# One 8 KB gather for both rows of an expert, and its gelu formed expert by expert

## The chip, the cores and the metric

The kernel runs on one core of a Trainium2 chip. The metric is the device time of one execution in microseconds (us); lower is better. Three runs of the kernel before took 3461.32, 3467.48 and 3471.10 us, the median is 3467.48 us.

## The reference

512 tokens of 1024 features in float32 go through three transformer blocks. The part that the change touches is the end of the second block, a layer of 16,384 experts of which every token uses 128 (8 heads times 16). Cut to that part:

```python
q  = (h @ wq).reshape(T, 8, 2, 128)
s1 = einsum('thd,hkd->thk', q[:, :, 0], keys1);  s2 = ...keys2
v1, i1 = top_k(s1, 16);  v2, i2 = top_k(s2, 16)        # per head
score, pos = top_k(all sums v1[i] + v2[j], 16)         # 16 of 256
ids   = take(i1 * 128 + i2, pos);   gates = softmax(score)
act   = gelu(einsum('pd,phkd->phk', h, expert_u[ids]))  # 128 dot products of 1024 per token
out   = einsum('phk,phkd->pd', gates * act, expert_v[ids])
```

`gelu` is the form with the hyperbolic tangent: 0.5 x (1 + tanh(0.79788 (x + 0.044715 x^3))). Each token needs 128 rows of `expert_u` and 128 rows of `expert_v`, each 4 KB, 512 x 256 x 4 KB = 537 MB in all.

## The kernel before

The 512 tokens are four tiles of 128, two to a half. The halves run one behind the other: while the experts of half 0 are gathered and summed, half 1 runs the rest of the first block and the mixer of the second; while the experts of half 1 run, half 0 runs its third block (`experts`, L1761). Weights come in 512 KB tiles over the SP queue into six buffers (`wtile`, L206). The experts of a half are a list of steps, `self.fill`. Whenever a phase of the other half asks for PSUM or a weight tile, `tick` (L130) adds credit and takes steps off the list, so that the expert steps are spread between the phase's instructions. This fixes one order of instructions, and each engine goes through its own part of it in that order. The pace is set by tables written out by hand (`ZONE`, `COURSE`), in which each expert step costs 1.46 units.

For one token tile, `gather_steps` (L1155) makes 256 steps: 128 u steps and 128 v steps. A step first calls `run_ahead`, which issues gathers up to 8 steps ahead (`AHEAD`). A gather (`fetch`, L1164) is an indirect DMA issued by GpSimd (POOL): 128 rows of 4 KB, one for each token, into one of the `GB` = 15 buffers named `gu`. Three of these hold other things: `h2` of the two tiles and the running sum `acc`.

A u step (L1171) is one VectorE (DVE) instruction that multiplies the gathered u rows with the activations `h2` and sums over 1024 into one column of `act`. After each 16 u steps (one head) ScalarE (ACT) takes the gelu of the 16 columns at once (L1174) and VectorE multiplies them with the gates (L1175). A v step adds c times the gathered v rows to the sum, c being a column of `act`: mostly VectorE does this (L1194); for a share of the steps that the phase sets, ScalarE builds a diagonal matrix `dg` from c (L1186, two buffers) and TensorE (PE) adds two products to PSUM (L1188). The order is 16 u steps, then u and v alternate with v 16 experts behind, then 16 v steps. `finish` (L1196) adds the two sums up and normalises.

The expert numbers and gates come from `route_steps` (L1242), two heads at a time; the softmax of the gates has an exp on ScalarE (L1294). `peer_route` (L1061) merges the steps of the routing with those of the experts.

Of the kernel before, what the change touches and what calls it, by code (L numbers as in the profile page):

```python
# [21 lines left out]
NT = 4          # token tiles  # L22
NH = 2          # token tiles of a half: the halves run one behind the other
# [34 lines left out]
class Ker:  # L58
    def __init__(self, ctx, tc, I):
# [3 lines left out]
        self.exact = False      # products in float32 itself, not in parts  # L63
# [14 lines left out]
        self.aux = nc.gpsimd        # for what VectorE need not do, unless GpSimd has transfers to start  # L78
# [3 lines left out]
        # states: of the first and of the second block, then both of the third block's retention  # L82
# [42 lines left out]
    def course(self, i):  # L125
        """the rate that spreads the steps of the experts over a phase"""
# [18 lines left out]
    def idle(self, d):  # L145
        """TensorE has little to do for d: pieces of the feed-forward set aside go in between"""
# [29 lines left out]
    def rsqrt(self, out, in_, scale, eps):  # L176
        """out = (in_ * scale + eps) ** -0.5: Newton's iteration from the halved exponent"""
# [43 lines left out]
    def ahead(self):  # L221
        """of the weights of a feed-forward set aside, split the next tile and load on"""
# [9 lines left out]
    def whole(gen):  # L232
        """all pieces of a generator at once; its value"""
# [12 lines left out]
    def g_fm(self, srcs):  # L246
        """feature-major blocks: out[f, i, t] = sum_k w_i[k, f] X[t, k]; srcs [128, 8*128]"""
# [16 lines left out]
    def g_tm(self, srcs, lhs, evac):  # L264
        """token-major: out[t, c] = sum_k lhs[k, t] w[k, c]; srcs: list of [128, 2, 512]; lhs(k) -> (H, L) [128, 512]"""
# [23 lines left out]
    def stats(self, y):  # L289
        """mean and variance over the free axis (1024 or 512)"""  # L290
# [12 lines left out]
    def g_transpose_x(self, src, scale=None, bias=None):  # L303
        """XH, XL <- split of (src^T * scale + bias); src(t, k) -> [128 t, 128 feat]"""
# [756 lines left out]
    def peer_route(self, rate):  # L1061
# [8 lines left out]
        with ExitStack() as e2:  # L1070
# [45 lines left out]
            def each(sc, h):  # L1116
# [5 lines left out]
                if h == 0:  # L1122
                    segs[0][0][0][2]()
# [31 lines left out]
    def gather_steps(self, t, y, h2, idx, gate):  # L1155
# [12 lines left out]
        def u_step(s, g):  # L1168
            if s == 0:
                begin()  # L1170
# [783 lines left out]
```

## Time and profile before

| | |
|---|---|
| median of three runs | 3467.48 us |
| span of the profiled execution | 3464.7 us, 44842 instructions |
| PE busy | 3023.7 us (87%) |
| DVE busy | 2667.9 us (77%) |
| POOL busy | 1439.0 us (42%) |
| ACT busy | 1145.3 us (33%) |
| DMA moved | 957.10 MB, mean 276 GB/s |

Busy time counts an engine's instructions, not the time in which it waits; a busy PE is not PE at its peak, since matmuls overlap. The profile gives no time for the profiled execution other than its span, which lies within the three runs. The expert stretch, from the first gather at 965 us to the last at 2861 us, is seen in the slices of the page: POOL is busy only there, and the DMA engines are at 0.9 or more in most slices of it.

### The profile page before, as it was taken

What the parts mean: (1) busy time and instruction counts of PE and PEld (TensorE: products, weight loads), DVE (VectorE), ACT (ScalarE), POOL (GpSimd) and SP (SyncE); (2) the same over time, 40 slices, a digit from 0 to 9 for tenths busy, and PEclk for the clock granted to TensorE, in tenths of its full rate; (3) what the DMA queues carried; (4) which work ended last, traced back from release to release, by engine and by line L of the source; (5) the groups of instructions that cost most, each with busy time, mean ns of one, the idle gap of its engine ahead of it and who ended that gap; (6) DMA issues with size and microseconds to landing.
All of it is one profiled execution on the core that took longest, in us unless ns stands there. A gap on an engine that the chain in (4) does not pass through costs nothing. (4 is left out here: it accounts for less than half of the span.)

```text
span 3464.7 us, 44842 instructions
## 1 busy us (share of the span) xinstructions
PE 3023.7 (87%) x15402; PEld 2350.9 (68%) x15402; DVE 2667.9 (77%) x6456; ACT 1145.3 (33%) x1687; POOL 1439.0 (42%) x1187
## 2 busy tenths in 40 slices
PE   9999999998979789987777867879797975999998
PEld 9987889888866357836354643536474745888897
DVE  7779686665588999878898999897877786566555
ACT  4454544553312242103222121112222213455554
POOL 0020000023245656655677567586767671211200
PEclk9999999999999899998899988899998987999999
DMA  8863477542389979998999899999999995644365
GB/s 312 279 194 118 131 267 233 168 161 86 105 303 357 355 263 384 409 402 325 381 326 375 335 339 391 347 368 357 333 365 359 396 409 193 182 133 139 119 188 162
DMA packets 276757, 957.10 MB, mean 276 GB/s; under 512 B 38304, under 2 KB 42144, under 8 KB 276528
## 3 DMA queue, kind: packets, MB, share of 16 engines
q0 software_dynamic: 147456, 536.94, 41.0%
q1 hardware_dynamic: 129072, 417.29, 35.6%
q8 instruction: 122, 2.00, 0.2%
q14 instruction: 107, 0.88, 0.1%
HBM read 947.81 MB, written 2.10 MB: 274 GB/s over the span
## 5 line engine op out<-in xcount | busy, mean ns | idle before, releaser
L1164 POOL DMA_INDIRECT gu<-in_peer_v,idx x512 | 633.6, 1238 | 317.1 <-issue 111.9
L1164 POOL DMA_INDIRECT gu<-in_peer_u,idx x512 | 609.3, 1190 | 349.6 <-issue 110.9
L1171 DVE SCALAR_TENSOR_TENSOR gu<-gu 128x1024 f32<-128x1024 f32 x512 | 620.7, 1218 | 59.4 <-DMA gu<-in_peer_u,idx 55.7
L203 DVE TENSOR_TENSOR wL<-wr,wH 128x1024 fp32r<-128x1024 f32 x332 | 409.1, 1234 | 249.2 <-ACT wH L202 231.9
L256 PE MATMUL ps<-XH,wr 128*128 128x256 f32 x2368 | 528.7, 383 | 0.2 <-issue 0.2
L256 PEld LDWEIGHTS ps<-XH,wr 128*128 128x128 f32 x2368 | 450.9, 192 | 73.2 <-issue 12.8
L202 ACT CAST wH<-wr 128x1024 fp32r<-128x1024 f32 x332 | 348.3, 1050 | 440.3 <-PE ps L281 217.4
L1194 DVE SCALAR_TENSOR_TENSOR gu<-gu,act 128x1024 f32<-128x1024 f32 x366 | 467.6, 1278 | 28.6 <-DMA gu<-in_peer_v,idx 23.4
L1188 PE MATMUL ps<-gu,dg 128*128 128x512 f32 x568 | 306.5, 664 | 101.8 <-DMA gu<-in_peer_v,idx 67.4
L1188 PEld LDWEIGHTS ps<-gu,dg 128*128 128x128 f32 x568 | 112.7, 212 | 206.9 <-issue 158.2
L278 PE MATMUL ps<-wr,XH 128*128 128x512 f32 x512 | 229.1, 601 | 0.0
L256 PE MATMUL ps<-XH,wH 128*128 128x256 f32 x1408 | 206.5, 289 | 16.3 <-ACT XH L116 10.0
L256 PE MATMUL ps<-XH,wL 128*128 128x256 f32 x1408 | 202.4, 287 | 1.5 <-DVE wL L203 1.2
L256 PE MATMUL ps<-XL,wH 128*128 128x256 f32 x1408 | 203.0, 288 | 0.2
L256 PEld LDWEIGHTS ps<-XH,wH 128*128 128x128 f32 x1408 | 186.6, 196 | 21.9 <-ACT XH L116 13.7
L256 PEld LDWEIGHTS ps<-XH,wL 128*128 128x128 f32 x1408 | 185.6, 196 | 2.9 <-DVE wL L203 2.7
L203 DVE TENSOR_TENSOR fL<-fr,fH 128x1024 fp32r<-128x1024 f32 x98 | 126.1, 1288 | 79.5 <-ACT fH L202 50.1
L256 PEld LDWEIGHTS ps<-XL,wH 128*128 128x128 f32 x1408 | 186.5, 197 | 0.6 <-DVE XL L118 0.6
L278 PEld LDWEIGHTS ps<-wr,XH 128*128 128x128 f32 x512 | 98.0, 193 | 122.7 <-issue 120.3
L202 ACT CAST fH<-fr 128x1024 fp32r<-128x1024 f32 x98 | 102.6, 1047 | 175.4 <-PE ps L256 58.7
L1186 ACT ACTIVATE dg<-ident,act 128x128 f32<-128x128 f32 x142 | 55.1, 400 | 312.3 <-PE ps L1188 246.5
L184 POOL TENSOR_TENSOR r<-rx,mhalf 128x1 f32<-128x1 f32 x18 | 11.9, 669 | 330.7 <-DVE rx L182 330.7
(618 smaller groups left out, 5462.4 us busy)
## 6 DMA issues: line engine op xcount, KB each, us to landing
wr<-in_wi_fm SPq DMA_DIRECT2D x112, 512.0 KB
wr<-in_wi_tm SPq DMA_DIRECT2D x96, 512.0 KB
wr<-in_wf SPq DMA_DIRECT2D x96, 512.0 KB
wr<-in_wo SPq DMA_DIRECT2D x64, 512.0 KB
wa<-in_wada SPq DMA_DIRECT2D x48, 512.0 KB
wr<-in_f2g SPq DMA_DIRECT2D x44, 512.0 KB
wr<-in_f2u SPq DMA_DIRECT2D x44, 512.0 KB
wr<-in_f2d SPq DMA_DIRECT2D x44, 512.0 KB
```

What stands on the lines that cost most here:

```text
L184: nc.gpsimd.tensor_tensor(out=out, in0=x, in1=self.mhalf[:p, :].to_broadcast(list(out.shape)), op=ALU.pow)
L202: self.nc.scalar.copy(H, raw)
L203: self.nc.vector.tensor_tensor(out=L, in0=raw, in1=H, op=ALU.subtract)
L256: nc.tensor.matmul(ps[:, i * TH:(i + 1) * TH], a[:, k * P:(k + 1) * P], b[:, k, :], start=n == 0, stop=n == KD * len(terms) - 1)
L278: nc.tensor.matmul(pss[t], lh[:, ts], wh, start=k == 0, stop=k == nk - 1)
L1164: nc.gpsimd.indirect_dma_start(out=g, out_offset=None, in_=I[src], in_offset=bass.IndirectOffsetOnAxis(ap=idx[:, s:s + 1], axis=0))
L1171: nc.vector.scalar_tensor_tensor(g, g, 1.0, h2, op0=ALU.mult, op1=ALU.mult, accum_out=st["act"][:, s:s + 1])
L1186: nc.scalar.activation(dg, self.ident, AF.Copy, scale=c)
L1188: nc.tensor.matmul(st["ps"][i], dg, g[:, i * 512:(i + 1) * 512], start="pe" not in st, stop=s == 127)
L1194: nc.vector.scalar_tensor_tensor(st["acc"], g, c, st["acc"], op0=ALU.mult, op1=ALU.add)
```

## The change

The two tables `expert_u` and `expert_v` are laid side by side on the host, one row of 8 KB for each expert. One gather brings both rows of an expert (128 rows of 8 KB, 1 MB), into one of 7 buffers of 8 KB for each partition; `h2` and `acc` have buffers of their own (`hb`, 4). `AHEAD` is 4 gathers.

The two tiles of a half are one list of 256 experts. Step u of expert i is followed by step v of expert i - 2 (`LAG`). The coefficient of each expert is formed by itself right after its u step: POOL multiplies the dot product x with the gate (`xg`), and ACT forms x squared, then x + 0.044715 x^3, the tangent, and c = xg (1 + th). The half that gelu needs goes into the gates: the sum of the softmax is doubled (one more VectorE instruction for two heads).

To make room, the tile `acc` of the first block's convolution is taken after the pool of `_hgrn` is closed, and the tiles `X3` of the third block are taken after `block3_mix` instead of before. The tables of the pace are the same. Comments are dropped.

```diff
-AHEAD = 8           # gathers under way ahead of their use
-GB = 15             # their buffers
+AHEAD = 4
+GB = 7
+LAG = 2
+GELU = (0.7978845608028654, 0.044715)
...
-        h2 = [pp.tile([P, D], F32, name="gu", bufs=GB) for _ in range(NH)]
+        h2 = [pp.tile([P, D], F32, name="hb", bufs=4) for _ in range(NH)]
...
-        def fetch(src, s):
-            g = pp.tile([P, D], F32, name="gu", bufs=GB)
-            nc.gpsimd.indirect_dma_start(out=g, out_offset=None, in_=I[src],
-                                         in_offset=bass.IndirectOffsetOnAxis(ap=idx[:, s:s + 1], axis=0))
-            return g
...
+        def fetch(i):
+            g = pp.tile([P, 2 * D], F32, name="gu", bufs=GB)
+            nc.gpsimd.indirect_dma_start(out=g, out_offset=None, in_=I["peer_uv"],
+                                         in_offset=bass.IndirectOffsetOnAxis(
+                                             ap=idx[i // P][:, i % P:i % P + 1], axis=0))
+            live[i] = [g, None]
+
+        def run_ahead(i):
+            while st.get("got", 0) <= min(i + AHEAD, NH * P - 1):
+                fetch(st.get("got", 0))
+                st["got"] = st.get("got", 0) + 1
...
-            nc.vector.scalar_tensor_tensor(g, g, 1.0, h2, op0=ALU.mult, op1=ALU.mult, accum_out=st["act"][:, s:s + 1])
-            if s % 16 == 15:
-                ah = st["act"][:, s - 15:s + 1]
-                nc.scalar.activation(ah, ah, AF.Gelu_apprx_tanh)
-                nc.vector.tensor_tensor(out=ah, in0=ah, in1=gate[:, s // 16, :], op=ALU.mult)
...
+        def u_step(i):
+            run_ahead(i)
+            t, s = divmod(i, P)
+            g = live[i][0]
+            a = pp.tile([P, 6], F32, name="ax", bufs=8)
+            x, q, z, th, xg, c = (a[:, k:k + 1] for k in range(6))
+            nc.vector.scalar_tensor_tensor(g[:, 0:D], g[:, 0:D], 1.0, h2[t], op0=ALU.mult, op1=ALU.mult, accum_out=x)
+
+            nc.gpsimd.tensor_tensor(out=xg, in0=x, in1=gate[t][:, s // 16, s % 16:s % 16 + 1], op=ALU.mult)
+            nc.scalar.activation(q, x, AF.Square, scale=math.sqrt(GELU[1]))
+            nc.scalar.activation(z, x, AF.Identity, scale=q, bias=x)
+            nc.scalar.activation(th, z, AF.Tanh, scale=GELU[0])
+            nc.scalar.activation(c, th, AF.Identity, scale=xg, bias=xg)
+            live[i][1] = c
...
+        steps, at = [], {}
+        for i in range(NH * P + LAG):
+            at[i] = len(steps)
+            if i < NH * P:
+                steps.append((DMA, lambda i=i: u_step(i)))
+            j = i - LAG
+            if j >= 0:
+                steps.append((DMA, lambda j=j: v_step(j)))
+                if j % P == P - 1:
+                    steps.append((FINISH, lambda t=j // P: finish(y[t])))
...
+            nc.vector.tensor_scalar(sm, sm, 2.0, None, op0=ALU.mult)
...
-    o["peer_u"], o["peer_v"] = n["peer_u_2"][0], n["peer_v_2"][0]
+    o["peer_uv"] = np.concatenate([n["peer_u_2"][0], n["peer_v_2"][0]], axis=1)
```

## Rows read from the trace of the kernel before

**Rows 1.** Stretches: length, busy us (count) by engine, PEclk, DMA share, GB/s.
```profile
1213.00:1300.00 87.00, 73.89 (x279) 49.33 (x278) 82.47 (x211) 37.92 (x83) 47.06 (x41) 0.92 0.75 264
...
1386.00:1473.00 87.00, 87.00 (x395) 74.71 (x394) 70.60 (x262) 13.75 (x18) 54.41 (x42) 1.00 1.03 409
...
953.00:2860.00 1907.00, 1585.88 (x6138) 1052.08 (x6136) 1653.23 (x4945) 412.18 (x759) 1241.52 (x1023) 0.91 0.95 358
```

**Rows 2.** DMA queues of the whole span: packets, MB, share of 16 engines.
```profile
q0 software_dynamic: 147456, 536.94, 41.0%
q1 hardware_dynamic: 129072, 417.29, 35.6%
q8 instruction: 122, 2.00, 0.2%
```

**Rows 3.** Costliest groups of the page: count, busy us, mean ns, idle before.
```profile
L1164 POOL DMA_INDIRECT gu<-in_peer_v,idx x512 | 633.6, 1238 | 317.1 <-issue 111.9
L1164 POOL DMA_INDIRECT gu<-in_peer_u,idx x512 | 609.3, 1190 | 349.6 <-issue 110.9
L1171 DVE SCALAR_TENSOR_TENSOR gu<-gu 128x1024 f32<-128x1024 f32 x512 | 620.7, 1218 | 59.4 <-DMA gu<-in_peer_u,idx 55.7
...
L1194 DVE SCALAR_TENSOR_TENSOR gu<-gu,act 128x1024 f32<-128x1024 f32 x366 | 467.6, 1278 | 28.6 <-DMA gu<-in_peer_v,idx 23.4
```

**Rows 4.** Waits from 1040 to 2860 us: total us, times, longest us.
```profile
ACT act L1174 <- DVE gu L1171: 253.8, 21, 56.5
ACT dg L1186 <- PE ps L1188: 228.9, 71, 13.0
...
POOL gu L1164 <- issue: 215.8, 644, 3.2
...
POOL gu L1164 <- DVE gu L1171: 77.0, 36, 12.5
...
DVE gu L1171 <- DMA gu<-in_peer_u,idx: 55.7, 46, 16.5
...
PE ps L1188 <- DMA gu<-in_peer_v,idx: 41.9, 9, 9.8
...
POOL gu L1164 <- DVE gu L1194: 34.2, 28, 4.3
...
POOL gu L1164 <- PE ps L1188: 31.6, 21, 4.4
...
DVE gu L1194 <- DMA gu<-in_peer_v,idx: 23.4, 34, 1.3
```

**Rows 5.** POOL in order of time: start, length us, idle before.
```profile
976.99 0.94 POOL L1164 DMA_INDIRECT gu<-in_peer_u,idx  x1 [0.30 <-issue]
```

**Rows 6.** Groups of instructions on ACT, shapes kept apart: count, busy us, mean ns.
```profile
L1174 ACT ACT_TABLE_LOAD x26 | 33.4, 1283 | 0.5
...
L1294 ACT ACT_TABLE_LOAD x14 | 18.0, 1283 | 0.2
...
L316 ACT ACTIVATE XH<-ps,bf,gf 128x256 f32<-128x256 f32 x16 | 7.5, 576 | 7.5 <-PE ps L310 7.5
...
L316 ACT ACTIVATE XH<-ps,n2w 128x256 f32<-128x256 f32 x8 | 3.4, 471 | 1.0 <-PE ps L310 1.0
...
L1428 ACT ACTIVATE mxo<-mxo,cb 128x16 f32<-128x16 f32 x12 | 3.1, 302 | 4.9 <-DVE mxo L1426 4.9
...
L878 ACT ACTIVATE bt<-ab 128x8 f32<-128x8 f32 x2 | 0.4, 208 | 0.0
```

**Rows 7.** Groups of instructions on POOL with few columns.
```profile
L184 POOL TENSOR_TENSOR r<-rx,mhalf 128x1 f32<-128x1 f32 x18 | 11.9, 669 | 330.7 <-DVE rx L182 330.7
...
L1058 POOL IOTA io<- 128x50 f32 x1 | 0.2, 187 | 0.0
```

**Rows 8.** The gates' multiplication on DVE, 1040 to 2860 us.
```profile
L1175 DVE TENSOR_TENSOR act<-act,gate 128x16 f32<-128x16 f32 x31 | 5.3, 170 | 4.5 <-ACT act L1174 4.5
```

More of the change, by code (lines that the diff above doesn't have):

```diff
@@ L467, in mixer1 @@
                 uT = cvp.tile([P, 4, 30 + TH], F32, name="uT")
-                acc = cvp.tile([P, 4, TH], F32, name="acc")
                 with ExitStack() as e3:
                     hp = e3.enter_context(tc.tile_pool(name="m1h", bufs=1))
-                    self._hgrn(hp, uT, acc)
-                self._conv31(cvp, uT, acc)
+                    self._hgrn(hp, uT)
+                with ExitStack() as e3:
+                    cvp = e3.enter_context(tc.tile_pool(name="m1a", bufs=1))
+                    self._conv31(cvp, uT, cvp.tile([P, 4, TH], F32, name="acc"))
             for c in range(2):
@@ L525, in _conv31, with _hgrn @@
         self.idle(GAP["l"])
-    def _hgrn(self, hp, uT, acc):
+    def _hgrn(self, hp, uT):
         nc, I = self.nc, self.I
@@ L1065, in peer_route @@
         self.rate, self.credit = rate, 0.0
-        h2 = [pp.tile([P, D], F32, name="gu", bufs=GB) for _ in range(NH)]
-        idx = [pp.tile([P, 128], U32, name=f"idx{t}") for t in range(NH)]
-        gate = [pp.tile([P, 8, 16], F32, name=f"gate{t}") for t in range(NH)]
-        segs = [self.gather_steps(t, self.x[:, self.tg(t), :], h2[t], idx[t], gate[t]) for t in range(NH)]
+        h2 = [pp.tile([P, D], F32, name="hb", bufs=4) for _ in range(NH)]
+        idx = [pp.tile([P, 128], U32, name=f"idx{t}", bufs=1 + t) for t in range(NH)]
+        gate = [pp.tile([P, 8, 16], F32, name=f"gate{t}", bufs=1 + t) for t in range(NH)]
+        segs, begin = self.gather_steps([self.x[:, self.tg(t), :] for t in range(NH)], h2, idx, gate)
         with ExitStack() as e2:
@@ L1122, in each @@
                 if h == 0:
-                    segs[0][0][0][2]()
+                    begin()
             nxt = scores(0, each)
@@ L1134, in peer_route @@
                         nxt = scores(1)
-                        self.fill += segs[0][0]
+                        self.fill += segs[0]
                         continue
                     rest[t].append(self.route_steps(g, sc[:, t, :, :], idx[t], gate[t]))
-        self.pop(len(self.fill) - len(segs[0][0]))
+        self.pop(len(self.fill) - len(segs[0]))
         u = self.merge(rest[0][1], self.fill)
         for g in (2, 3):
-            u += self.merge(rest[0][g], segs[0][g - 1])
-        last = segs[0][3][-17:]
-        u += self.merge(sum(rest[1], []), segs[0][3][:-17])
-        b = sum(segs[1], [])
-        self.fill = u + [f for p in zip(last[:16], b[:16]) for f in p] + b[16:20] + last[16:] + b[20:]
+            u += self.merge(rest[0][g], segs[g - 1])
+        self.fill = u + self.merge(sum(rest[1], []), segs[3]) + segs[4]
     @staticmethod
@@ L1180, in v_step @@
                 st["ps"] = [self.psum(), self.psum()]
-            c = st["act"][:, s:s + 1]
+                st["pe"] = False
             self.vcredit += self.vshare
-            if (self.vcredit >= 1.0 and s) or s == 127:
+            if (self.vcredit >= 1.0 and s) or s == P - 1:
                 self.vcredit -= 1.0
@@ L1186, in v_step @@
                 nc.scalar.activation(dg, self.ident, AF.Copy, scale=c)
-                for i in range(2):
-                    nc.tensor.matmul(st["ps"][i], dg, g[:, i * 512:(i + 1) * 512],
-                                     start="pe" not in st, stop=s == 127)
+                for k in range(2):
+                    nc.tensor.matmul(st["ps"][k], dg, g[:, k * 512:(k + 1) * 512],
+                                     start=not st["pe"], stop=s == P - 1)
                 st["pe"] = True
@@ L1208, in finish @@
             nc.vector.scalar_tensor_tensor(y, y, r, fw, op0=ALU.mult, op1=ALU.mult)
-        order = [(u_step, "peer_u", s) for s in range(16)]
-        for h in range(8):
-            for k in range(16):
-                if h < 7:
-                    order.append((u_step, "peer_u", 16 * (h + 1) + k))
-                order.append((v_step, "peer_v", 16 * h + k))
-        ahead = []
-        def run_ahead(i):
-            while len(ahead) < len(order) and len(ahead) <= i + AHEAD:
-                ahead.append(fetch(*order[len(ahead)][1:]))
-        def step(i):
-            run_ahead(i)
-            order[i][0](order[i][2], ahead[i])
-            ahead[i] = None
-        steps = [(DMA, lambda i=i: step(i)) for i in range(len(order))] + [(FINISH, finish)]
-        steps[0] += (lambda: run_ahead(0),)
-        cut = [0, 48 - 2 * AHEAD, 112 - 2 * AHEAD, 176 - 2 * AHEAD, len(steps)]
-        return [steps[a:b] for a, b in zip(cut, cut[1:])]
+        steps, at = [], {}
[8 more added lines that the diff above has]
+                    steps.append((FINISH, lambda t=j // P: finish(y[t])))
+        cut = [0] + [at[32 * k - AHEAD] for k in (1, 2, 3, 4)] + [len(steps)]
+        return [steps[a:b] for a, b in zip(cut, cut[1:])], lambda: run_ahead(0)
     def top16(self, src, val, idx, n):
@@ L1783, in experts @@
             last = self.ctx.enter_context(ExitStack())
-            self.exact = False
-            self.xt(last, "right")
-            X3 = self.XH, self.XL
-            self.exact = True
             with ExitStack() as es:
@@ L1790, in experts @@
                 self.block3_mix()
+                X = self.XH, self.XL
+                self.exact = False
+                self.xt(last, "right")
+                X3 = self.XH, self.XL
+                self.exact = True
+                self.XH, self.XL = X
                 self.zone("F3")
```

21 lines of the change are left out of this document (10 added, 11 removed).

## Prediction

> **What bounds the kernel now.** First the stretches. Gathers run from 953 to 2860 us, and only this part is changed; the 953 us before it and the 605 us behind it keep their instructions. In the 1907 us of it [rows 1] the DMA engines have a share of 0.95, DVE is busy 1653 us (87%), PE 1586 us (83%), POOL 1242 us (65%), ACT 412 us (22%). No engine has room of more than a few per cent beside the DMA and DVE. Single slices go both ways: one at 0.75 of DMA with DVE busy 82 of 87 us, one at 1.03 of DMA and 409 GB/s with PE busy throughout [rows 1].
>
> Next the waits of the stretch, read for who waits for a gather [rows 4]. DVE waits for u rows 55.7 us and for v rows 23.4 us, PE for v rows 41.9 us, together 121 us. POOL, which issues the gathers, waits in its turn for buffers that DVE and PE still hold: 77.0 + 34.2 + 31.6 = 143 us. (These waits are of 1040 to 2860 us.) So neither side leads: the gathers are a little late about as often as the buffers are. Faster gathers can return 121 us and no more, for the rest of DVE's 254 idle us (1907 - 1653) is other waits. ACT, the idlest, is told apart by what it waits for: 254 us at the gelu for a u step of DVE, 229 us at `dg` for PE. It runs ahead of both, and little waits for it.
>
> **The change part by part.** The sum is made against the span, 3464.7 us; the median of the runs is 2.8 us above it, and that is added at the end.
>
> *Gathers.* 1024 of 512 KB become 512 of 1 MB; the bytes stay 537 MB. On POOL a gather takes 1238 or 1190 ns [rows 3], at best 0.94, with 0.30 us of issue before it [rows 5]. If an 8 KB row costs POOL what a 4 KB row costs, 512 x (1.21 + 0.30) = 773 us leave POOL; if its work goes by 4 KB pieces, only 512 x 0.30 = 154 us. I take the first, since the instruction names 128 rows in both. POOL's work isn't on the path by itself; its relief is worth what of the 121 us comes from late issue. For the DMA engines, a packet of q0 costs 41.0% x 16 x 3464.7 us / 147456 = 154 ns for 3.6 KB on average, and one of q8 with 16 KB about 909 ns (0.2% of the same sum over 122) [rows 2]: larger packets are not seen to move bytes faster, so bounds are 0 and the whole 121 us. With the share at 0.95 and equal bytes I take a third: -40 us.
>
> The Trainium skill would say more: DMA: Bandwidth & Descriptors, section "Anatomy of one DMA", gives a fixed 2.0 us and bytes at 436 GB/s for each DMA, and its rules ask for 1 MiB. By that a gather of 512 KB alone runs at about 163 GB/s and one of 1 MB at 238 (estimates from the page). The trace disagrees: with 512 KB gathers and 512 KB weight tiles the engines reached 409 GB/s [rows 1], since the fixed parts lie beside other transfers.
>
> *Depth of the gathers.* Before, 15 - 3 = 12 buffers: a gather waits for the step 12 earlier, 11 steps of 1907 / 1024 = 1.86 us lie between. Now gather i + 4 waits for v of expert i - 3, after which 8 steps come before it is used. The lead falls by 3 steps, 5.6 us. If the 143 us of buffer waits grow by 3/11 it costs 39 us, if the DMA queue stays filled 0; I take +10, nearer to zero, because with a share of 0.95 four gathers and the weights keep the engines in work.
>
> *The chain of c.* Four ACT instructions and one on POOL for each expert, 512 times. A narrow activation takes 208 ns, with one pointer operand 302 ns for 16 columns; a second pointer costs 576 - 471 = 105 ns [rows 6]. Square and tangent 0.2 each, the two with two pointers 0.4 each: 1.2 us, 614 us of ACT in all, which brings it to about 53%. The product on POOL lies between 0.19 (the 50-column iota) and 0.67 us (a one-column power) [rows 7]; I take 0.5. It is queued behind the gather issued just before, which waits for v of i - 3, one DVE step before u of i ends; 0.30 + 1.21 + 0.5 - 1.22 = 0.8 us after u, beside the first three of ACT. So c is there some 1.2 to 1.6 us after its u step. For DVE this is covered: v of i starts after v, u, v, u. TensorE takes 512 - 366 - 4 = 142 of the v steps [rows 3], so the four take 2 x 1.22 + 2 x 0.72 x 1.28 = 4.3 us, and 2.7 us of cover are left.
>
> What is queued behind the waiting instruction on ACT isn't covered. ACT ran ahead of DVE by a whole head of 16 experts (its 254 us of waits came in 21 pieces [rows 4]); now it stops at each u step, and the PSUM copies and activations of the phases stand behind. Of ACT's 759 instructions in the stretch [rows 1] some 32 + 40 + 142 are the experts' own (gelu, table loads, `dg`), 545 are the phases'. An expert comes each 1907 / 512 = 3.7 us, so 1.6 / 3.7 = 0.43 of them fall behind a chain and lose half of it, 0.8 us: 188 us of lateness. It counts where PE or DVE has nothing else queued; as their share I take how much of the stretch they idle, 17 + 13 = 30%: +56 us. The bounds are 0 (all hidden by queued work) and +188.
>
> *The wait at `dg`.* ACT waits 229 us in 71 pieces for PE to release `dg`, 3.2 us each, the longest 13.0 [rows 4]. Now the c of later experts stand behind that wait; before, they had been formed up to 16 experts ahead. Past the cover of 2.7 us I take a third, 76 us, and 30% of that: +23 us. Bounds 0 and 229.
>
> *Table loads.* The gelu brought 26 loads and the exp behind it 14, 1.283 us each, 51 us of ACT [rows 6]. They go. Which loads the tangent brings, the trace can't show: from none to a pair for each expert, 512 x 2 x 1.283 = 1314 us. The nearest row is the gelu's own; as many loads as before, 0, is what I take. The Trainium skill (ScalarE: Activation LUTs, "Table sets: the hidden batching unit") puts tanh into the sets of exp and of sigmoid, by which the 51 us would mostly go; at 30% that would be 15 us off the sum.
>
> *DVE and the rest.* 32 gate products of 170 ns go [rows 8], 5.4 us; 16 doublings of about the same length come, 2.7 us: -3 us. u and v steps are the same instructions on the same elements. The later `acc` and `X3` cost nothing: each is written only after the phase whose space it takes, in the order of the code before; if that cover were gone, one phase boundary would show. The number of steps and their price in `fill` are the same, so the pace between phases stays.
>
> Sum: -40 + 10 + 56 + 23 + 0 - 3 = +46 us; 3464.7 + 46 + 2.8 = 3513 us.
>
> **The rivals.** *Gathers set the pace (faster).* POOL with its issue time is occupied (1242 + 216) / 1907 = 76% and waits for buffers besides; with half the instructions gathers leave on time, and the chain hides as ACT is half idle. Half of the 121 us and the 3 us: 3467 - 63 = 3404 us; all of it, 3343. For it: DVE does wait for gathers, in pieces up to 16.5 us [rows 4]. Against it: the DMA share. The skill's 1 MiB rule, taken at its word, would land here as well.
>
> *The DMA sets the time (no change).* Bytes and packets' price stay, the share is 0.95, and every delay of ACT lies beside transfers: 3467 within 10. Against it: slices such as the one at 0.75, where DVE is the full engine.
>
> *ACT ties PE and DVE together (much slower).* Place: the ACT queue, where c of an expert, `dg` and the copies of the phases stand in one line; it waits for DVE at each u and for PE at each copy. From the point where c comes later than the 2.7 us of cover, DVE stops, buffers stay taken and the gathers stop with it. Half of 188 + 229 us comes through, and the gathers gain nothing: 3467 + 209 = 3676 us. For it: ACT's waits for PE have a mean of 3.2 us, above the cover. Against: PE and DVE are already kept together by the phases.
>
> *An 8 KB row counts as two (the change halves nothing).* POOL then takes up to 0.94 us more for each gather, the product on POOL comes later and c at 2.5 us; the chain term becomes 0.3 x 545 x 0.68 x 1.25 = 139, the gain zero: 3467 + 139 + 23 + 10 - 3 = 3636 us. The q8 row speaks neither for nor against it.
>
> *Table loads at each expert.* ACT would need 412 + 614 + 1314 = 2340 us, more than the stretch: 3467 + 433 = 3900 us.
>
> **How the numbers follow.** Forecast (slower, 3480 to 3565 us) 0.33; tied queues 0.06; double rows 0.05; table loads 0.03: slower 0.47. No change 0.14. Faster 0.39, most of it near 3404. The bound of 0.3% (10 us) is about what a measurement of this kernel can tell from no change. The forecast's own range is 3480 to 3565. For eight in ten the range goes down past the faster rival to 3385, where a tenth is left for more of the 121 us, and up to 3610, where a tenth is left for the tied queues and the last two rivals.
>
> **What would show it.** In the changed kernel's profile: 512 gathers on POOL with a mean near 1.2 us (near 2 if rows count as two); DMA packets of q0 halved or not; DVE's waits for `gu` smaller by about 40 us; ACT near 1030 us busy in the stretch, with a wait of short pieces for L1171's successor in place of the 21 long ones; new waits of DVE's v step and of `dg` for c if the cover is too short; waits of PE and DVE for phase copies of ACT longer by 50 to 80 us. The prediction is wrong if those waits stay as they are, or if the DMA share stays at 0.95 while the stretch becomes shorter than 1907 us: then the transfers themselves became cheaper.

## The result and the profile after

The changed kernel takes 3681.53 us (median of four runs, 3675.76 to 3683.09) against 3469.29 us for the kernel before on the same chip: ratio 1.0618 [1.0593, 1.0642], 6.2% slower. The forecast (3513 us) had the sign, not the size: the time lies above the forecast's own range (3480 to 3565 us) and above the wider one (3385 to 3610 us).

First, where in the span the time went. The first u step and the last v step of VectorE mark the expert stretch; these are lines of the views by source line, for the kernel before and then for the changed one (after the count: duration min/median/max in ns, then first and last start in us).

```profile
L1171 DVE SCALAR_TENSOR_TENSOR gu<-gu x512: 1160/1216/1273, 984.4 to 2852.1; 128x1024 f32<-128x1024 f32 x171
L1194 DVE SCALAR_TENSOR_TENSOR gu<-gu,act x366: 1176/1277/1321, 1039.9 to 2878.4; 128x1024 f32<-128x1024 f32 x183
```

```profile
L1178 DVE SCALAR_TENSOR_TENSOR gu<-gu,hb x512: 1154/1218/1301, 1010.0 to 3092.2; 128x1024 f32<-128x1024 f32 x171
L1207 DVE SCALAR_TENSOR_TENSOR hb<-gu,ax,hb x361: 1161/1279/1331, 1032.1 to 3094.8; 128x1024 f32<-128x1024 f32 x181
```

The first u step comes 25.6 us later, the stretch from there to the last v step grows from 1894.0 to 2084.8 us (+190.8), and what follows is as before (586.3 and 584.2 us). The sum is 214.3 us, the difference of the spans (3679.0 - 3464.7). The instructions themselves did not become slower: medians of 1216 and 1218, 1277 and 1279 ns.

The whole stretch of the changed kernel, with columns as in [rows 1]:

```profile
953.00:3080.00 2127.00, 1668.04 (x6293) 1089.98 (x6291) 1677.71 (x4966) 841.40 (x2732) 934.62 (x1026) 0.88 0.85 324
```

Over the stretch the DMA share fell from 0.95 to 0.85 and the rate from 358 to 324 GB/s [rows 1]. VectorE's share fell from 87% to 79% (1677.71 of 2127), TensorE's from 83% to 78%, GpSimd's from 65% to 44%. No resource became the full one; more waits lie between them. TensorE's granted clock in the stretch, a mean over its two levels of 2.4 and 1.2 GHz, went from 0.91 [rows 1] to 0.88 of full speed; how much of the loss comes through the clock no run tells apart. The queues and the costliest groups of the page, which answer to [rows 2, 3]:

```profile
q0 software_dynamic: 73728, 536.90, 38.1%
q1 hardware_dynamic: 129072, 417.29, 33.1%
...
L1162 POOL DMA_INDIRECT gu<-in_peer_uv,idx x512 | 664.4, 1298 | 873.9 <-DVE hb L1207 381.4
L1178 DVE SCALAR_TENSOR_TENSOR gu<-gu,hb 128x1024 f32<-128x1024 f32 x512 | 623.4, 1220 | 190.2 <-DMA gu<-in_peer_uv,idx 184.1
...
L1181 ACT ACTIVATE ax<-ax 128x1 f32<-128x1 f32 x512 | 103.1, 202 | 870.3 <-DVE gu L1178 869.5
L1180 POOL TENSOR_TENSOR ax<-ax,gate 128x1 f32<-128x1 f32 x512 | 263.5, 517 | 305.8 <-DVE gu L1178 216.5
...
L1182 ACT ACTIVATE ax<-ax 128x1 f32<-128x1 f32 x512 | 194.5, 380 | 8.3
L1184 ACT ACTIVATE ax<-ax 128x1 f32<-128x1 f32 x512 | 189.4, 376 | 10.6 <-POOL ax L1180 6.5
```

There are 512 gathers of 1298 ns on GpSimd and half the packets of before (147456 [rows 2]). The bytes cost the DMA engines what they did: 38.1% of 16 x 3679.0 us over 73728 packets is 304 ns each, against 154 ns for half the size. The waits in the stretch (1040 to 3080 us), read as [rows 4]:

```profile
ACT ax L1181 <- DVE gu L1178: 838.4, 388, 11.2
POOL gu L1162 <- DVE hb L1207: 381.2, 191, 25.2
...
POOL gu L1162 <- PE ps L1201: 202.9, 73, 11.9
POOL ax L1180 <- DVE gu L1178: 202.0, 51, 18.0
...
DVE gu L1178 <- DMA gu<-in_peer_uv,idx: 180.8, 146, 5.5
PE ps L1201 <- ACT dg L1199: 157.9, 41, 13.7
...
DVE hb L1207 <- ACT ax L1184: 71.7, 105, 3.7
...
POOL ax L1180 <- DVE rt L192: 68.1, 2, 67.2
```

Three things are new against [rows 4]. GpSimd waits 202.0 + 68.1 us at the product `xg`, a time in which it issues no gather. TensorE waits 157.9 us for ScalarE's `dg`; before it was ScalarE that waited there for TensorE, 228.9 us. And VectorE, which was to wait less for gathers, waits 180.8 us for them where it waited 55.7 + 23.4.

### The profile page after: what moved, and what is told of

The parts are those of the page before. It is cut to its first block, busy times and chain, and to the rows that moved or that the text cites. A ratio compares the mean times of both kernels' runs of the same rounds, so it can differ in the third digit from the quotient of the medians.

```text
span 3679.0 us, 47053 instructions
## 1 busy us (share of the span) xinstructions
PE 3081.3 (84%) x15422; PEld 2368.3 (64%) x15422; DVE 2672.7 (73%) x6435; ACT 1568.1 (43%) x3662; POOL 1123.6 (31%) x1187
## 3 DMA queue, kind: packets, MB, share of 16 engines
q0 software_dynamic: 73728, 536.90, 38.1%
## 5 line engine op out<-in xcount | busy, mean ns | idle before, releaser
L1162 POOL DMA_INDIRECT gu<-in_peer_uv,idx x512 | 664.4, 1298 | 873.9 <-DVE hb L1207 381.4
L1178 DVE SCALAR_TENSOR_TENSOR gu<-gu,hb 128x1024 f32<-128x1024 f32 x512 | 623.4, 1220 | 190.2 <-DMA gu<-in_peer_uv,idx 184.1
L205 DVE TENSOR_TENSOR wL<-wr,wH 128x1024 fp32r<-128x1024 f32 x332 | 410.3, 1238 | 268.3 <-ACT wH L204 251.0
L1201 PE MATMUL ps<-gu,dg 128*128 128x512 f32 x588 | 344.0, 713 | 207.9 <-ACT dg L1199 195.8
L1207 DVE SCALAR_TENSOR_TENSOR hb<-gu,ax,hb 128x1024 f32<-128x1024 f32 x361 | 461.4, 1278 | 74.2 <-ACT ax L1184 73.5
L1181 ACT ACTIVATE ax<-ax 128x1 f32<-128x1 f32 x512 | 103.1, 202 | 870.3 <-DVE gu L1178 869.5
L1180 POOL TENSOR_TENSOR ax<-ax,gate 128x1 f32<-128x1 f32 x512 | 263.5, 517 | 305.8 <-DVE gu L1178 216.5
L1201 PEld LDWEIGHTS ps<-gu,dg 128*128 128x128 f32 x588 | 121.4, 222 | 341.0 <-ACT dg L1199 229.0
L1182 ACT ACTIVATE ax<-ax 128x1 f32<-128x1 f32 x512 | 194.5, 380 | 8.3
L1184 ACT ACTIVATE ax<-ax 128x1 f32<-128x1 f32 x512 | 189.4, 376 | 10.6 <-POOL ax L1180 6.5
```

The lines of the kernel that those rows point to most:

```text
L205: self.nc.vector.tensor_tensor(out=L, in0=raw, in1=H, op=ALU.subtract)
L1162: nc.gpsimd.indirect_dma_start(out=g, out_offset=None, in_=I["peer_uv"], in_offset=bass.IndirectOffsetOnAxis(ap=idx[i // P][:, i % P:i % P ...
L1178: nc.vector.scalar_tensor_tensor(g[:, 0:D], g[:, 0:D], 1.0, h2[t], op0=ALU.mult, op1=ALU.mult, accum_out=x)
L1180: nc.gpsimd.tensor_tensor(out=xg, in0=x, in1=gate[t][:, s // 16, s % 16:s % 16 + 1], op=ALU.mult)
L1181: nc.scalar.activation(q, x, AF.Square, scale=math.sqrt(GELU[1]))
L1182: nc.scalar.activation(z, x, AF.Identity, scale=q, bias=x)
```

## The experiments

Ratios are to the kernel before, run beside it on the same chip, with 95% intervals. "us" made from a ratio is the ratio less 1, times 3467. Four kernels (e2, e7, e9, e18) leave the gelu out and multiply the v rows with the gate alone; e3 and e16 form c but use the gate.

### The later space of acc

**e5**, the kernel before with this one edit, and **e6**, the changed kernel without it:

```diff
 # e5
-                acc = cvp.tile([P, 4, TH], F32, name="acc")
...
-                self._conv31(cvp, uT, acc)
+                with ExitStack() as e3:
+                    cvp = e3.enter_context(tc.tile_pool(name="m1a", bufs=1))
+                    self._conv31(cvp, uT, cvp.tile([P, 4, TH], F32, name="acc"))
 # e6
+                acc = cvp.tile([P, 4, TH], F32, name="acc")
...
-                    self._conv31(cvp, uT, cvp.tile([P, 4, TH], F32, name="acc"))
+                    self._conv31(cvp, uT, acc, late)   # only sq and rs in the later pool
```

> The kernel before with one part of the change alone: the tile acc of the convolution (and its small tiles) taken after the pool of the first mixer is closed. The changed kernel's first gather comes at 1000 us instead of 965, with the convolution's first products on VectorE at 385 instead of 254 us. Theory 3: the later acc costs this by itself, since the convolution can't be drawn forward into the mixer's gaps: 35 us in half 0, and more in half 1, which runs beside the experts: 3500 to 3580 us beside some 3455 of the kernel before. Theories 1 and 2 (chain, buffers) alone: within 10 us of the kernel before.

> The changed kernel with acc taken early again, as before (only two 1 KB tiles of the convolution's norm stay late to make room). Theory 3: 70 to 130 us come back, 3540 to 3600 us beside 3670 of the changed kernel on this chip. If only half 0 matters: 3630 us. Chain alone: unchanged.

e5: 3540.28 us, 1.0197 [1.0162, 1.0232]. e6: 3620.13 us, 1.0448 [1.0405, 1.0492], against 1.0618 with the edit. So the edit costs 1.7 to 2.0%, 59 to 68 us, either way round. The place is seen in the convolution's products, by source line, for before and for the changed kernel:

```profile
L500 DVE SCALAR_TENSOR_TENSOR acc<-uT,cw,acc x180: 460/471/1518, 253.5 to 1260.0; 128x256 f32<-128x256 f32 x180
```

```profile
L503 DVE SCALAR_TENSOR_TENSOR acc<-uT,cw,acc x180: 466/471/485, 384.6 to 1356.4; 128x256 f32<-128x256 f32 x180
```

In the code they stand behind `_hgrn`. In the kernel before, VectorE nevertheless starts them at 253.5 us, ahead of instructions of `_hgrn` that follow from 304.7 us on (L627), and beside the mixer's products on TensorE; with the space of `_hgrn` still taken they start at 384.6 us. The section on the kernel before has each engine go through its part in the order of the code; these starts show that it does not. Two windows show what that means, before and then after:

```profile
253.00:300.00 47.00, 44.47 (x275) 39.03 (x274) 47.00 (x89) 19.88 (x24) 3.41 (x3) 1.00 0.54 161
390.00:433.00 43.00, 42.24 (x265) 38.34 (x264) 24.21 (x32) 22.91 (x31) 0.00 (x0) 0.97 0.44 134
```

```profile
253.00:300.00 47.00, 45.99 (x278) 40.03 (x277) 24.00 (x27) 24.80 (x30) 3.69 (x3) 1.00 0.61 197
390.00:433.00 43.00, 23.31 (x128) 20.82 (x126) 43.00 (x99) 8.16 (x8) 0.00 (x0) 0.76 0.21 67
```

The work that lay beside TensorE's now lies by itself: VectorE is full from 390 to 433 us and TensorE half idle, its granted clock 0.76 on average against 0.97. In half 1, inside the expert stretch, the products move behind `_hgrn` too: they start at 1333.0 us, after its last L630 at 1309.5, where before they started at 1146.3 us and its last L627 came at 1228.5. In e6 the products run from 252.1 us again and the first u step comes at 971.6 us (after: 1010.0).

### The chain taken out or left unused

**e2** takes the chain out of the changed kernel; **e3** forms it, but v takes the gate; **e7** is e2 with acc early.

```diff
 # e2, e7
-            nc.gpsimd.tensor_tensor(out=xg, in0=x, in1=gate[t][...], op=ALU.mult)
-            nc.scalar.activation(q, x, AF.Square, ...)
...
 # e2, e3, e7
-            live[i][1] = c
+            live[i][1] = gate[t][:, s // 16, s % 16:s % 16 + 1]
```

> The changed kernel without the chain: the four activations and the product on POOL are left out and v takes the gate itself as its coefficient (so the gelu and the factor x are missing from the output). The 8 KB gathers, their order and their buffers stay. Theory 1 (the chain): near the kernel before or below, 3400 to 3490 us. Theory 2 (the buffers): 3600 to 3680 us, since the gathers are as they were.

> The changed kernel with the chain formed on ACT and POOL as it is, but the v step takes the gate as its coefficient and doesn't wait for c (the gelu is missing from the output). If what costs is that ACT stops at each u step with the copies of the phases behind it: as the changed kernel, 3620 to 3690 us. If what costs is the wait of v and dg for c: as the kernel without the chain. If the buffers: 3600 to 3680 us in both.

> The same with the chain left out as well (v takes the gate, the gelu is missing from the output). The kernel without the chain alone was 3.4% above the kernel before. If chain and acc are the whole of it: within 1% of the kernel before, 3430 to 3490 us. If the 8 KB buffers or the new order cost something of their own: 3500 us or more.

e2: 3567.24 us, 1.0340 [1.0314, 1.0366]. e3: 3589.31 us, 1.0386 [1.0366, 1.0406]. e7: 3509.33 us, 1.0125 [1.0088, 1.0162]. From e6 to e7 the chain is worth 3.2%, 112 us, the largest part of the loss. At this lag most of the price goes already when v no longer needs c: e3 costs 0.5% over e2, though all the chain's instructions are still there.

### The size of the gathers

**e1** is the changed kernel with two gathers of 4 KB in 14 buffers, eight ahead; **e9** is e7 with them.

```diff
-            g = pp.tile([P, 2 * D], F32, name="gu", bufs=GB)
-            nc.gpsimd.indirect_dma_start(out=g, ..., in_=I["peer_uv"], ...)
+            g = pp.tile([P, D], F32, name="gu", bufs=2 * GB)
+            nc.gpsimd.indirect_dma_start(out=g, ..., in_=I["peer_" + k], ...)
```

> The changed kernel (3682 us) with its order, its lag of 2 experts and its chain of c, but with separate gathers of 4 KB rows for u and v, in 14 buffers of 4 KB (the same memory), issued 8 gathers ahead. Theory 1, the chain: forming c for each expert by itself ties ACT, PE and DVE to each u step; then this stays near the changed kernel, 3630 to 3720 us. Theory 2, the buffers: an 8 KB buffer holds the u half until the v step is done, so the gathers leave later and the DMA engines run dry; then the 4 KB buffers, whose u half comes free 4 steps sooner, bring it back to 3450 to 3530 us.

> acc early and no chain, as the last but one of the runs before (1.25% above the kernel before), and with separate gathers of 4 KB rows in 14 buffers. If the rest of 1.25% is the 8 KB buffers, held until the v step: within 0.4% of the kernel before, 3450 to 3480 us beside some 3466. If it is the order of the steps (one list for both tiles, v 2 experts behind u): it stays 0.8 to 1.6% above. The gelu is missing from the output.

e1: 3672.07 us, 1.0615 [1.0585, 1.0645], the same as with 8 KB. e9: 3475.26 us, 1.0057 [1.0041, 1.0073], below e7's 1.0125 [1.0088, 1.0162]. So the larger gather gave nothing with the chain, and without it the smaller one is better by 0.7%, 24 us. The 0.6% that e9 still costs, without a gelu, is left for the new order of steps, the later `X3` and the buffers of `h2` and `acc`; it wasn't taken apart.

### The lag

```diff
 # e4: lag 1, five ahead     e8: lag 3, three ahead     e12: e9 with the chain and lag 8
-AHEAD = 4
-LAG = 2
+AHEAD = 5
+LAG = 1
```

> The changed kernel with a lag of 1 expert instead of 2 and gathers 5 ahead instead of 4: v of an expert comes two steps sooner after its u, so c has less time, but a gather's buffer is free two steps sooner and the gathers have a lead of 10 steps instead of 8. Theory 1 (the chain): slower than the changed kernel, 3720 to 3900 us. Theory 2 (the buffers): faster, 3550 to 3650 us.

> The changed kernel with a lag of 3 experts and gathers 3 ahead: c has two more steps of time, a gather's lead falls from 8 steps to 6. A lag of 1 cost 3.6% more. If the wait for c decides: faster than the changed kernel, 3590 to 3640 us. If the lead of the gathers decides by now: slower, 3690 to 3760 us.

> The changed kernel's chain of c, with acc early and separate 4 KB gathers, and v 8 experts behind u instead of 2; with separate buffers the lag costs none. If the shortness of the lag is what the chain costs: 0 to 1.5% above the kernel before, 3465 to 3520 us. If ACT's stops at each u are: 3 to 4.5% above, 3570 to 3620 us.

e4: 3795.53 us, 1.0995 [1.0974, 1.1016]. e8: 3631.22 us, 1.0467 [1.0433, 1.0501]; the kernel with lag 2 has 1.0618. e12: 3563.34 us, 1.0304 [1.0269, 1.0339]. One expert less costs 3.8%, one more gives 1.5%, in both cases with the gathers ahead changed the other way by one; yet eight experts with 4 KB gathers still leave 2.5% over e9. Lag alone does not explain the chain's price.

### Table loads

**e11** is the kernel before with the gelu of a head formed from the tangent, 16 columns at once (for each head one instruction more on ScalarE and two more on VectorE).

```diff
-                nc.scalar.activation(ah, ah, AF.Gelu_apprx_tanh)
+                nc.scalar.activation(q, ah, AF.Square, scale=math.sqrt(0.044715))
+                nc.vector.scalar_tensor_tensor(q, q, 1.0, ah, op0=ALU.add, op1=ALU.mult)
+                nc.scalar.activation(q, q, AF.Tanh, scale=0.7978845608028654)
...
+                nc.vector.scalar_tensor_tensor(ah, q, 1.0, ah, op0=ALU.add, op1=ALU.mult)
```

> The kernel before with the gelu of a head formed from the tangent (one square and one tangent on ACT, three small instructions on VectorE instead of one): only the function is changed. If the tangent needs no table load of its own beside exp and sigmoid: the 26 loads at the gelu and most of the 14 behind it go, some 50 us of ACT, and the time is 0 to 0.6% lower. If it brings as many loads: the same, or up to 0.3% slower for the 11 us of VectorE.

3458.96 us, 1.0026 [1.0017, 1.0036]. The 26 loads at the gelu go and those at the exp fall from 14 to 8, and the time does not fall. Whether the added instructions eat up a small gain isn't parted.

### Which part of the chain costs

**e10** puts the chain into the kernel before: its order, 4 KB gathers and 16 experts between u and v stay. **e13** is e10 with the product on ScalarE, **e16** is e10 with v on the gate.

```diff
 # e10
-            nc.vector.scalar_tensor_tensor(g, g, 1.0, h2, ..., accum_out=st["act"][:, s:s + 1])
-            if s % 16 == 15:
...
+            nc.gpsimd.tensor_tensor(out=xg, in0=x, in1=gate[...], op=ALU.mult)
+            nc.scalar.activation(q, x, AF.Square, scale=math.sqrt(0.044715))
+            nc.scalar.activation(z, x, AF.Identity, scale=q, bias=x)
+            nc.scalar.activation(th, z, AF.Tanh, scale=0.7978845608028654)
+            nc.scalar.activation(c, th, AF.Identity, scale=xg, bias=xg)
 # e13
-            nc.gpsimd.tensor_tensor(out=xg, in0=x, in1=gate[...], op=ALU.mult)
+            nc.scalar.activation(xg, x, AF.Identity, scale=gate[...])
```

> The kernel before, order and 4 KB gathers and 16 experts between u and v kept, with the gelu formed for each expert by the chain on POOL and ACT instead of once for a head. If the chain costs because ACT stops at each u step: 1.5 to 3% slower, 3515 to 3570 us. If it costs because c is needed so soon after its u step: within 0.7% of the kernel before, 3450 to 3490 us.

> The kernel before with its 4 KB gathers, its order and its lag of 16 experts, and the chain of c formed for each expert as in the run that put this chain into it (3522.05 us, ratio 1.0205), but with x times gate as a fifth instruction of ScalarE in place of GpSimd's. Theory 1 (GpSimd is the price: the product stands in the same queue as 1024 gathers, holds them up while it waits for VectorE, and fills GpSimd to 88% with its issue time): the ratio falls to 1.003 to 1.008, and the waits of VectorE and TensorE for gathers, 351 us with the product on GpSimd, fall back toward the 147 us of before. Theory 2 (ScalarE is the price: it now stops at each u step, and copies of the phases stand behind): ScalarE does more than there, 512 x 0.3 us, so the ratio stays at 1.02 or rises to 1.025. Theory 3 (c comes late for the v step): with 16 experts between it cannot, no change against before beyond 0.3%.

> The kernel before with the chain of c formed for each expert on GpSimd and ScalarE (ratio 1.0205), but the v step takes the gate in place of c: the gelu's result is left out of the sum, the instructions stay. Theory 1 and theory 2 (the chain's place in the queues of GpSimd or ScalarE is the price): 1.017 to 1.022, with gathers as late as there. Theory 3 (the price is that v and dg wait for c): 1.000 to 1.006, and ScalarE's waits before dg return to TensorE's release.

e10: 3522.05 us, 1.0205 [1.0190, 1.0221]. e13: 3495.24 us, 1.0086 [1.0069, 1.0102]. e16: 3539.84 us, 1.0212 [1.0195, 1.0230]. With this lag the need for c costs nothing (e16 is like e10): the chain's place in the queues does. GpSimd's product alone is 1.2% (e10 to e13). The waits of e10 (1040 to 2920 us) and of e13 (1040 to 2890 us) show whom it holds up:

```profile
ACT ax L1176 <- DVE gu L1174: 557.6, 280, 16.8
...
DVE gu L1174 <- DMA gu<-in_peer_u,idx: 112.2, 83, 15.0
PE ps L1192 <- DMA gu<-in_peer_v,idx: 108.7, 27, 17.8
DVE gu L1198 <- DMA gu<-in_peer_v,idx: 53.4, 60, 2.6
POOL ax L1175 <- DVE gu L1174: 40.9, 22, 4.5
```

```profile
ACT ax L1175 <- DVE gu L1174: 428.7, 244, 21.9
...
DVE gu L1174 <- DMA gu<-in_peer_u,idx: 57.2, 48, 16.0
...
DVE gu L1198 <- DMA gu<-in_peer_v,idx: 29.4, 40, 2.0
...
PE ps L1192 <- DMA gu<-in_peer_v,idx: 27.8, 10, 6.4
```

Waits for gathers are 274 us with the product in GpSimd's queue and 114 us without, about the 121 us of before [rows 4]. Behind the product stand the gathers of later experts: while it waits for its u step, and while it runs, none is issued. The two stretches, again e10 and then e13, show how little room GpSimd has for that with 1024 gathers:

```profile
953.00:2900.00 1947.00, 1598.08 (x6112) 1052.63 (x6112) 1646.29 (x4913) 831.92 (x2703) 1533.85 (x1516) 0.90 0.93 347
```

```profile
953.00:2900.00 1947.00, 1594.60 (x6127) 1059.58 (x6125) 1658.84 (x4926) 987.69 (x3248) 1229.14 (x1024) 0.90 0.94 352
```

It is busy 1533.85 of 1947 us in e10 (79%), to which 177.8 us of issue come (1040 to 2920 us), and 1229.14 us in e13. The 0.9% left in e13 was not taken apart; ScalarE stops there 244 times at a u step, 428.7 us in all.

**e14** and **e15** are e6 with the product on ScalarE, with lag 2 and with lag 3 and three ahead. **e17** is e15 with ScalarE's gelu, two instructions for five; **e18** is e15 without the chain.

```diff
 # e14, e15
-            nc.gpsimd.tensor_tensor(out=xg, in0=x, in1=gate[t][...], op=ALU.mult)
+            nc.scalar.activation(xg, x, AF.Identity, scale=gate[t][...])
 # e17, in place of all five
+            nc.scalar.activation(xg, x, AF.Gelu_apprx_tanh)
+            nc.scalar.activation(c, xg, AF.Copy, scale=gate[t][...])
```

> The changed kernel with the convolution's acc taken early (3620.13 us, ratio 1.0448), and x times gate as a fifth instruction of ScalarE in place of GpSimd's. Theory 1 (the product in GpSimd's queue makes the gathers late): 1.025 to 1.03, and GpSimd's waits at the product, 182 us and 78 us, are gone. Theory 2 (ScalarE's stops and the short way from u to v): the chain becomes longer by 0.3 us and the lag is still 2 experts, so 1.045 to 1.055; the waits of TensorE and its weight load for dg (195 and 228 us) stay or grow.

> The same as the run beside it with the product on ScalarE, and v three experts behind u instead of two, with three gathers ahead instead of four. Theory 2 (short way from u to v): 1.3 to 1.8% below the run beside it, as lag 3 was 1.5% below lag 2 with the product on GpSimd; the waits for dg fall by half. Theory 1 (GpSimd): with the product gone from its queue, one gather less ahead decides, and the time is the same or up to 0.5% longer.

> The version with acc early, the product on ScalarE and lag 3 (3554.97 us, ratio 1.0254), with ScalarE's own gelu for each expert and one multiplication with the gate in place of the five instructions: about 0.5 us of ScalarE for an expert in place of about 1.46. If what is left of the chain's price is its length on ScalarE (c late for dg and copies of the phases behind it): 1.014 to 1.019, TensorE's waits for dg (163 and 197 us) fall by half. If the price is that ScalarE stops at each u step at all, whatever the length: 1.022 to 1.026. If gelu brings a table load whenever a phase has used another function (26 loads in the kernel before), there are some hundred loads of 1.28 us and the gain is gone: above 1.025.

> The same version (acc early, 8 KB gathers, lag 3) without any chain: v takes the gate in place of c, and the gelu is left out. With lag 2 this was 1.0125. If the short way from u to v costs only through the chain, lag 3 without it is the same, 1.010 to 1.014; if the buffers of 8 KB that stay taken until v are the price of what is left, one more expert held and one gather less ahead make it 1.013 to 1.018.

e14: 3564.84 us, 1.0295 [1.0276, 1.0313]. e15: 3554.97 us, 1.0254 [1.0234, 1.0273]. e17: 3549.98 us, 1.0212 [1.0176, 1.0248]. e18: 3512.96 us, 1.0109 [1.0075, 1.0144]. The waits of e6 (1040 to 3020 us) and then of e14 (1040 to 2970 us), which differ in the place of the product alone:

```profile
POOL gu L1162 <- DVE hb L1207: 316.6, 163, 9.4
...
POOL gu L1162 <- PE ps L1201: 197.6, 72, 11.6
...
DVE gu L1178 <- DMA gu<-in_peer_uv,idx: 181.6, 149, 5.8
POOL ax L1180 <- DVE gu L1178: 157.6, 47, 17.8
PE ps L1201 <- ACT dg L1199: 155.7, 39, 14.4
```

```profile
POOL gu L1162 <- DVE hb L1207: 508.0, 165, 20.4
POOL gu L1162 <- PE ps L1201: 349.4, 94, 75.9
...
PE ps L1201 <- ACT dg L1199: 163.6, 44, 13.9
...
DVE gu L1178 <- DMA gu<-in_peer_uv,idx: 70.8, 52, 5.8
```

Without the product GpSimd stands ready earlier (it waits 508 + 349 us for buffers, where it waited 317 + 198), and VectorE's waits for gathers fall from 181.6 to 70.8 us: 1.5% of the time, 53 us, though ScalarE's part became longer. With 512 gathers GpSimd is not full (934.62 of 2127 us in the changed kernel), so the reason differs from e10's. Rows and runs fit a ring: a gather waits for the buffer that v frees, the product stands behind that gather, c needs the product, and v needs c. e14 opens the ring at the product, e3 at v. In e3 (1040 to 3000 us) GpSimd waits even longer at the product, and VectorE waits less for gathers all the same:

```profile
POOL ax L1180 <- DVE gu L1178: 586.1, 260, 23.8
...
DVE gu L1178 <- DMA gu<-in_peer_uv,idx: 110.9, 95, 4.4
```

That it is this ring is argued from the two runs, not measured by itself. The lag is worth 0.4% here, not the 1.3 to 1.8% expected, so most of what lag 3 gave in e8 seems to have been room for GpSimd's product. TensorE's waits for `dg` stay at 163.6 us in e14. In e18 ScalarE has no u step to stop at, and it is ScalarE again that waits for TensorE at `dg`, 416 us in 111 pieces. Shortening the chain does not bring that back. In e17 ScalarE's groups are these:

```profile
L1181 ACT ACTIVATE ax<-ax,gate 128x1 f32<-128x1 f32 x512 | 147.9, 292 | 12.9
L1180 ACT ACT_TABLE_LOAD x81 | 103.9, 1283 | 1.5
L1180 ACT ACTIVATE ax<-ax 128x1 f32<-128x1 f32 x512 | 102.8, 203 | 856.6 <-DVE gu L1178 850.7 <-issue 3.8 <-DVE mxc L1421 0.8
```

ScalarE's 765 us of busy time between 953 and 2990 us are 241 less than in e15, but TensorE still waits 158.2 us for `dg` (953 to 3060 us), and the ratio is 0.4% below e15's, with intervals that overlap. Of the 1.45% that the chain still costs at lag 3 (e15 over e18) the larger part, about 1.0%, thus stays with two instructions in place of five. That part goes with ScalarE's stop at each u step, but the runs don't part the stop from what else e17 has: v still needs c, and the gelu brings 81 table loads, 103.9 us. What the length of the chain costs by itself these runs don't settle.

## Why the prediction was wrong

The loss, split by the runs in which one thing at a time was undone (from ratios, in us of 3467):

| part | runs | cost |
|---|---|---|
| later space of `acc` | changed, e6 | 1.7%, 59 us |
| product on GpSimd | e6, e14 | 1.5%, 53 us |
| rest of the chain, on ScalarE | e14, e7 | 1.7%, 59 us |
| 8 KB gathers and their buffers | e7, e9 | 0.7%, 24 us |
| left (order of steps, later `X3`, buffers of `h2` and `acc`) | e9 | 0.6%, 20 us |

The parts add up to the whole because each run is compared with the next; undone in another order they come out otherwise (`acc` 2.0% by e5, the product 1.2% by e10 and e13). By the intervals of the ratios each is good to some 6 to 17 us (an estimate). e7 and e9 have no gelu at all, so the price of the chain is counted from nothing, and the kernel before pays for its own gelu.

*Later acc: +0 forecast, +59 measured.* This is the step that failed outright: "each is written only after the phase whose space it takes, in the order of the code before". The term was put at nothing, and what the runs showed in its place is 59 to 68 us: with its space free early the convolution runs on VectorE beside `_hgrn`, and with the later space it has to follow. It acts ahead of the stretch too, which the prediction took as unchanged there (the first u step comes 25.6 us later). That the order of the code is not the order on an engine stood in the trace of before, in the start of L500. It was not looked up, since the edit seemed to touch nothing. The named alternative, "one phase boundary would show", had the place and no number. For the later `X3` no run was made alone; the part after the last v step didn't grow.

*Chain of c: +56 for the copies of the phases and +23 at `dg`, 79 forecast, 112 measured.* The durations were right: 202 + 380 + 201 + 376 ns = 1.16 us on ScalarE (1.2 forecast), 0.52 us on GpSimd (0.5). What failed first is the sentence that put the product "beside the first three of ACT". It asked what the product waits behind (the gather), and not what waits behind the product: the next gathers. That is 53 us, nearly half of this cost (e6 to e14; in the other kernel e10 to e13).

The other half, 59 us (e14 to e7), is near the 79 forecast, but not by the two places forecast; that the sizes are close is luck. The +56 stood for TensorE and VectorE waiting longer for ScalarE's copies for the phases. Their waits for all of ScalarE's results other than `dg`, the gelu and the chain came to 76 and 44 us before (1040 to 2860 us) and to 94 and 37 us in the changed kernel (1040 to 3080 us), 18 us more and 7 less where 50 to 80 had been named; the prediction had said "The prediction is wrong if those waits stay as they are". The +23 was to come from ScalarE standing at `dg` until TensorE releases it, 229 us before. That wait all but vanished, and TensorE waits for `dg` instead, 157.9 us. So ScalarE's stop at each u step did hold up what stands behind it, as forecast, but that was `dg` and not the copies, and at `dg` the wait turned round. The first line is from the waits of ScalarE in the changed kernel (953 to 3080 us), the other two show a `dg` in ScalarE's queue right behind a square (L1181) that had to wait for a u step:

```profile
ACT dg L1199 <- PE ps L1201: 8.3, 4, 3.2
```

```profile
1024.29 0.20 ACT L1181 ACTIVATE ax<-ax 128x1 f32<-128x1 f32 x1 [2.36 <-DVE gu L1178]
1024.40 0.39 ACT L1199 ACTIVATE dg<-ident,ax 128x128 f32<-128x128 f32 x1
```

Without the chain (e7) ScalarE waits 513.2 us for TensorE there again (1040 to 2900 us).

The cover of 2.7 us between u and v was used up by order, too. Three instructions of ScalarE in the changed kernel in order of time, and then a v step of VectorE that waits for the c among them (start, length in us, idle before):

```profile
1509.60 0.20 ACT L1181 ACTIVATE ax<-ax 128x1 f32<-128x1 f32 x1 [2.77 <-DVE gu L1178]
1509.71 0.37 ACT L1184 ACTIVATE ax<-ax 128x1 f32<-128x1 f32 x1
1509.98 0.37 ACT L1182 ACTIVATE ax<-ax 128x1 f32<-128x1 f32 x1
```

```profile
1510.11 1.28 DVE L1207 SCALAR_TENSOR_TENSOR hb<-gu,ax,hb 128x1024 f32<-128x1024 f32 x1 [0.55 <-ACT ax L1184]
```

The last step of an earlier expert's chain (L1184) stands behind the square (L1181) of a later one, which waits for its u step; its own z and tangent had been formed before. So c comes only 0.5 us after a u step of another expert, and VectorE waits 0.55 us for it. In all, VectorE waits for c 105 times, 71.7 us; how many of these have this cause was not counted.

*Gathers: -40 forecast, nothing gained.* Half the instructions, hardly longer (1298 ns against 1190 and 1238), and half the packets: the mechanism "an 8 KB row costs POOL what a 4 KB row costs" held. But GpSimd's relief was worth nothing, since it spent the time waiting for buffers (e7: 432 us for VectorE's, 260 us for TensorE's). The 121 us of waits for gathers were not lateness of issue: with half the instructions and no chain VectorE and TensorE still wait 75.6 + 60.3 = 136 us for them (e7, 1040 to 2900 us). The Trainium skill's rule to batch DMAs to 1 MiB or more (DMA: Bandwidth & Descriptors, section "Bandwidth"), which the prediction set against the trace, is not borne out here. Gathers of 1 MB came to 1.0618 and those of 512 KB (e1) to 1.0615, and without the chain to 1.0125 (e7) and 1.0057 (e9).

*Depth: +10 forecast.* With the 8 KB buffer held from u to v, 24 us (e7 to e9, which changes size and depth together).

*Table loads: 0 forecast.* The forecast took as many loads as before; that was wrong, but the size was right. The 26 at the gelu went, the tangent brought 2 (L1183), and those at the exp fell from 14 to 5. e11, in which most of these loads go as well, shows no gain, though with 64 small VectorE instructions in exchange. The Trainium skill (ScalarE: Activation LUTs, "Table sets: the hidden batching unit") has tanh in the sets of exp and of sigmoid, and the trace agrees, with 2 loads for 512 tangents. That the loads' going is worth 15 us, as the prediction worked out beside it, does not show.

*The rivals.* "Gathers set the pace" and "the DMA sets the time" fell with the share at 0.85. "An 8 KB row counts as two" and "table loads at each expert" fell with the 1298 ns of a gather and with the 2 loads at the tangent. "ACT ties PE and DVE together" gave 3676 us, close to the time, but by luck: its place, ScalarE's queue, accounts for 59 us of the 212.

No version beat the kernel before; the nearest were e11 (1.0026) and, without the gelu, e9.

## What to carry to other kernels

For a small instruction put into an engine's queue ask both questions: what it waits for, and what stands behind it on that engine while it waits; if those are issues of transfers, it is paid in lateness of data elsewhere. Before costing a moved allocation at nothing, look up in the trace when the first instruction that writes it starts, and against which instructions of the phase whose space it would take. A stage made expert by expert in place of sixteen at a time ends an engine's running ahead, and here that lead was the cover, not the engine's idle share.

## What the hardware showed

A gather of 128 rows costs GpSimd about the same for 8 KB rows (1298 ns) as for 4 KB rows (1190 and 1238 ns [rows 3]), and the DMA engines the same time for the same bytes (304 ns for a packet against twice 154 ns). The one-column product on GpSimd has a mean of 517 ns with a spread from 184 to 2875 ns; on ScalarE one-column instructions have means of 201 and 202 ns, or 376 and 380 ns with two pointer operands.
